# A hybrid SSD / short-convolution block on one core: group-wise scratch tensors, joined transfers, stores on another queue, and a new order at two turns

## The chip, the cores and the metric

The kernel runs on one core of a Trainium2 chip. The metric is device time in microseconds (us), the median of several executions. All arithmetic is float32; matrix products are made of three passes over operands that are split into a high and a low part.

## What is computed

The input x is 1024 tokens by 1024 channels. Cut to what matters here, the reference is:

```python
u = rmsnorm(x) @ w_in                    # 9248 columns in all
z, xbc, dt_raw, s_b, s_c, s_x, g_a, g_b = split(u)
xbc = silu(causal_conv4(xbc) + bias)     # xs 2048, B 4x128, C 4x128
y = ssd_chunked_scan(xs, softplus(dt_raw + bias), a, B, C) + d_skip * xs
y = group_rmsnorm(y * silu(z)) * w       # 4 groups of 512 channels
branch_a = y @ w_ssd_proj
branch_b = (s_b * causal_conv3(s_c * s_x)) @ w_sconv_proj
h = x + (sigmoid(g_a) * branch_a + sigmoid(g_b) * branch_b) @ w_o
h = h + (silu(n(h) @ w_gate) * (n(h) @ w_up)) @ w_down
out = rmsnorm(h)
```

## The kernel before, in words

The order of the instructions on each engine is the order of the program text: nothing is moved by a scheduler. Every wait is a semaphore wait of an engine that works in order. DMAs are issued from three queues: SP's (nearly all loads and most stores), ACT's (a few stores) and POOL's (transfers that add into their target). Working tiles are 47 equal pages of on-chip memory; a new tile takes a page whose last user stands earlier in the program, and waits for that user. Some DMAs also wait for an earlier transfer with other data to land before they are issued (the fourth load of x does): they share a semaphore with it.

The work comes in five stages.

**Start** (`hybrid_block`, lines 225 to 262 and 1487 to 1593). Four row tiles of x are loaded, their squares are summed, the rows are scaled (`rows_scale`, line 129) and transposed on PE; the small weights (`ra`, `rb`) are loaded, transposed (lines 1533 and 1534) and copied into `cols`. Rows 4 to 7 follow as `r1`.

**Pairs.** `x @ w_in` is made in pairs of 128-column blocks, each pair with seven products in place of eight (`Pair`, line 829). A pair has seven slots; a slot is 12 matmuls of 128x512. Operands of x are held as `T["B11"]`, `T["B21"]`, `T["B22"]` and the sums `T["T1"]` to `T["T4"]`. Results go through `silu_z` or `conv_silu`, which run as generators in the list `side`, one step a slot (`pump`), and are stored to DRAM (`z_d`, `xbc_d`) from SP's queue. Meanwhile `weight_sums` makes sums of later weights by DMA alone. `time_steps` (line 286) is the chain for dt; its generator `rest` starts with one empty step.

**Direct tiles with the scans.** The last 22 column blocks (6 of z, 16 gates) are made by `direct_tile` (line 989), 16 turns of three matmuls each, so 352 turns. Between them runs the generator `scans` (line 557), one step each time `pump_scan` is called: first the loads of the first scan inputs (`want`, `prep`), then for each of the 32 items (4 groups by 8 chunks) `part1` and `part2`, 65 steps in all. Each half group ends in a `norm` generator (line 498) of 15 or 18 further steps, advanced one by one with the scan's steps: load of z, product on POOL, squares on ACT, sums on DVE, column sums on PE (`pq`, line 523), the root, a transpose on PE (`prt`, line 528), a small store and a broadcast load back (`rs_d`, `rbc`, lines 532 and 534), scaling (line 540), stores, and for a second half four sums with their stores (line 553).

Ahead of the turn from the pairs to the direct tiles, the loop at line 1652 counts `left`, the slots still to come: at 9 it loads `B12` back, at 8 it makes the scan's first step (the loads), at 6 it loads the first direct slab, at 2 it loads the second, splits the first (`direct_hi`), drops `T2` and starts to split `B12`, at 1 it finishes both and makes the scan's second step. In the direct tiles a scan step is due every 322/65 turns; in the last 30 turns there is a step every third turn, and `every(scan_steps)` runs what is left of the last norm before the next stage.

**Merge and output.** `ms` (line 1158) streams chunks of three products: `gv` (14 chunks), `gy` (28), `go`. A chunk is 24 matmuls; loads run four chunks ahead, splits two. `Merge.first` loads and squashes the gates.

**FFN** (`ffn_phase`) is not touched.

Of the kernel before, what the change touches and what calls it, by code (L numbers as in the profile page):

```python
# [8 lines left out]
F32 = mybir.dt.float32  # L9
# [30 lines left out]
def hybrid_block(ctx: ExitStack, tc: tile.TileContext, x, nmw, w_in, cw, cb, dtb, alog, dsk, snw,  # L40
# [193 lines left out]
    ra = cp.tile([96, P], F32, name="ra")  # L234
    nc.scalar.dma_start(ra, cw[0].rearrange("k (i p) -> (k i) p", p=P))
    rb = cp.tile([80, P], F32, name="rb")
    nc.scalar.dma_start(rb[0:8, :], nmw.rearrange("o (i p) -> (o i) p", p=P))
    nc.scalar.dma_start(rb[8:16, :], nfw.rearrange("o (i p) -> (o i) p", p=P))
    nc.scalar.dma_start(rb[16:40, :], cb.rearrange("o (i p) -> (o i) p", p=P))
    nc.scalar.dma_start(rb[40:56, :], snw.rearrange("o (i p) -> (o i) p", p=P))  # L240
    nc.scalar.dma_start(rb[56:80, :], scw[0].rearrange("k (i p) -> (k i) p", p=P))

# [8 lines left out]
    def small_loads():  # L251
        nc.sync.dma_start(d2, dsk.rearrange("o (i j) -> (o i) j", j=2))
        nc.sync.dma_start(dtbc, dtb.rearrange("o h -> h o"))
        for q in range(4):
            nc.sync.dma_start(al[32 * q:32 * q + 32, :], alog.rearrange("o h -> h o"))
    rd = cp.tile([16, 2, 64], F32, name="rd")
# [11 lines left out]
    e_d = dr.tile([NT, H, P], F32, name="e_d")  # L268
    xbc_d = [dr.tile([P, S], F32, name=f"xbc_d{i}") for i in range(24)]
    z_d = [dr.tile([P, S], F32, name=f"z_d{i}") for i in range(16)]  # L270
    b12_d = dr.tile([2, P, 2, 512], F32, name="b12_d")
    y_g = [dr.tile([512, S], F32, name=f"y_g{i}") for i in range(G)]
    v_g = [dr.tile([512, S], F32, name=f"v_g{i}") for i in range(2)]
    y_d = [y_g[i // 4][i % 4 * P:i % 4 * P + P, :] for i in range(16)]
    v_d = [v_g[i // 4][i % 4 * P:i % 4 * P + P, :] for i in range(KT)]
    ga_d = [dr.tile([P, S], F32, name=f"ga_d{i}") for i in range(KT)]
    gb_d = [dr.tile([P, S], F32, name=f"gb_d{i}") for i in range(KT)]
    rs_d = [dr.tile([4, P], F32, name=f"rs_d{i}") for i in range(2 * G)]
# [7 lines left out]
    def time_steps(ps):  # L286
# [13 lines left out]

        def rest():
            yield
            V.scalar_tensor_tensor(e, u, -1.0, u, op0=ALU.mult, op1=ALU.max)
# [48 lines left out]
    def want(i, part):  # L352


        if i < 2 * G:
            g, o = i // 2, i % 2 * 512
            bcx = [xbc_d[16 + g], xbc_d[20 + g]] + xbc_d[4 * g:4 * g + 4]
            if part < 2:
                t = page("bc", (P, 4, 256))
                for j in range(4):  # L360
                    nc.sync.dma_start(t[:, j, :], bcx[j][:, o + part * 256:o + part * 256 + 256])
            else:
                t = page("x1", HB)
                for j in range(2):
                    nc.sync.dma_start(t[:, j, :], bcx[4 + j][:, o:o + 512])
            halves[i, part] = t
# [131 lines left out]
    def norm(g, hf, y0, y1):  # L498

        ys, o = (y0, y1), slice(hf * 512, hf * 512 + 512)  # L500
        for i in range(2):
            z = page("z", HB)
            for r in range(2):
                nc.sync.dma_start(z[:, r, :], z_d[4 * g + 2 * i + r][:, o])
            if i == 0:
                zs = z
# [31 lines left out]
        for r in range(4):  # L538
            z = ys[r // 2][:, r % 2]
            V.scalar_tensor_tensor(z, z, snc(4 * g + r), rbc, op0=ALU.mult, op1=ALU.mult)  # L540
            if hf == 0 or r > 1:
                nc.sync.dma_start(y_d[4 * g + r][:, o], z)
            if r % 2:
                yield
        if hf == 0:
            kept[g] = ys
            return
# [41 lines left out]
    def conv_silu(i):  # L589

        def f(u):
# [9 lines left out]
            nc.scalar.activation(acc, acc, AF.Silu)  # L601
            nc.sync.dma_start(xbc_d[i], acc)
            yield
        return f

    def silu_z(i):
        def f(u):
            nc.scalar.activation(u, u, AF.Silu)
            nc.sync.dma_start(z_d[i], u)
            yield  # L610
        return f
# [377 lines left out]
    def direct_tile(i):  # L989
# [3 lines left out]
        for hf in range(2):  # L993
            ps = bank("pr")
            for k in range(KT):
                bh, bl = half_b(f"B{k // 4 + 1}{hf + 1}", k % 4)
                mm3(ps, wh[:, k, :], wl[:, k, :], bh, bl, k == 0, k == KT - 1)
                turn[0] += 1
                due = turn[0] * SCAN_STEPS // (len(direct) * 2 * KT - 30)
                if turn[0] > len(direct) * 2 * KT - 30:  # L1000
                    pump_scan(turn[0] % 3 == 0)
                elif due > turn[1]:
                    turn[1] = due
                    pump_scan()
# [13 lines left out]
    class Merge:  # L1018
# [5 lines left out]
        def first(self, c):  # L1024
            n = c.n
            if n not in (2, 7, 3, 4):
                return
            i, j = TO[n]
            if c.k == 0:
                self.g[i, j] = [page("gt", HB) for _ in range(2)]  # L1030
                for m in range(4):
                    nc.sync.dma_start(self.g[i, j][m // 2][:, m % 2, :], self.gd[4 * i + m][:, j * 512:j * 512 + 512])
# [54 lines left out]

    mv = Merge(gb_d, None)
    my = Merge(ga_d, mv.c)

# [9 lines left out]

    def act_blk(d, at):
        def f(f, k, n):
            l, j = int(f[1]) - 1, int(f[2]) - 1

            def ld(t):
                for i in range(n):
                    nc.sync.dma_start(t[:, i, :], d[at(l, k) + i][:, j * 512:j * 512 + 512])
            return ld
        return f

    def fb_v(f, k, n):
        return wfrm(vt_d, f, k, n) if f[0] == "T" else act_blk(v_d, lambda l, k: 4 * l + k)(f, k, n)

    def fb_y(f, k, n):
        return wfrm(yt_d, f, k, n) if f[0] == "T" else act_blk(y_d, yk)(f, k, n)

# [418 lines left out]
    nc.vector.tensor_copy(cols[:, 0:176], pc[:, 0:176])  # L1535
    r0 = rows_scale(*a0, act=(2,), pool=(3,))
    raw0, raw1 = ([], []), ([], [])
# [42 lines left out]
    for k in range(4, 8):  # L1580
        turned_out(raw0, k)
    p1.ev(1)
    every(put("B21", raw0[1]))
    r1 = rows_scale(*a1, act=(2,), pool=(3,))
    p2.ev(1)
# [66 lines left out]
    for i in range(7 * NF, n_slots):  # L1652
# [13 lines left out]
        left = n_slots - 1 - i  # L1666
        if left == 6:
            direct[0][0].load()
        if left == 8:
            pump_scan()  # L1670
        if left == 2:
            direct[1][0].load()
            direct_hi(direct[0][0])
            del T["T2"]
            b12_put = put("B12", b12)
            next(b12_put)
        if left == 9:
            b12 = [page("br", HB) for _ in range(2)]
            for k in range(2):
                nc.sync.dma_start(b12[k], b12_d[k])  # L1680
        if left == 1:
            every(b12_put)
            direct_lo(direct[0][0])
            pump_scan()
    every(sums)
    for f in ("T1", "T3", "T4"):
        del T[f]
    del b12
# [40 lines left out]
```

## Time and profile before

| | us |
|---|---|
| median of 3 runs | 1953.3 |
| lowest, highest | 1949.79, 1953.45 |
| the profiled execution's own time | 1949.93 |
| its span, first to last instruction | 1948.2 |

The page gives each engine's busy time, the granted TensorE clock in 40 slices, the DMA queues and the costliest groups; the views used below are the list of waits (who waited for whom, in total, number of times and longest), the busy time of each engine in a stretch, and the timeline of an engine (start, duration, engine, line, operation, tiles, count, and in brackets the idle time before it and what ended it). Matmul records overlap: one lasts 0.39 us at the full clock while the next starts 0.23 us later.

### The profile page before, as it was taken

How to read it: one execution, taken by the hardware profiler on the slowest of the kernel's cores; microseconds unless marked ns; L12 is line 12 of the kernel's file. 1: busy time of each engine (PE TensorE's matmuls, PEld its weight loads, DVE VectorE, ACT ScalarE, POOL GpSimd, SP SyncE). 2: the span in 40 equal slices, each digit the busy share in tenths (PEclk: the TensorE clock that was granted, in tenths of full speed). 3: DMA queues.
4: the chain of work that ended last, by engine and by line, in shares of the span. 5: the costliest groups of instructions: out<-in, count | busy, mean ns of one | idle time of the engine just before them, and what ended most of it. 6: DMA issues, size and time to landing. Idle time of an engine off the chain costs nothing.

```text
span 1948.2 us, 24338 instructions
## 1 busy us (share of the span) xinstructions
PE 1891.2 (97%) x8917; PEld 1553.1 (80%) x8917; DVE 1291.0 (66%) x1658; ACT 965.8 (50%) x1536; POOL 179.5 (9%) x158
## 2 busy tenths in 40 slices
PE   6999999999997999999989999999999999999998
PEld 5678888888885887888768888888888888888886
DVE  6757877777773778887766557878444444456465
ACT  5545444444445888777546445365333333335333
POOL 0001111011100111011100000101121112100000
PEclk9999999999998999999999999999999999999999
DMA  5187999899957667877778666845988888868552
GB/s 169 37 213 201 224 238 215 232 241 233 260 159 220 190 208 234 268 242 239 227 286 320 213 206 203 224 156 110 232 195 192 213 199 200 207 252 302 195 188 114
DMA packets 347120, 411.99 MB, mean 211 GB/s; under 512 B 19112, under 2 KB 225784, under 8 KB 347000
## 3 DMA queue, kind: packets, MB, share of 16 engines
q1 hardware_dynamic: 300288, 343.23, 54.2%
q0 software_dynamic: 43296, 55.58, 17.8%
q10 hardware_dynamic: 3416, 11.63, 1.5%
q8 instruction: 70, 1.15, 0.2%
q14 instruction: 50, 0.41, 0.1%
HBM read 320.56 MB, written 143.15 MB: 238 GB/s over the span
## 4 chain that ended last, share of the span: by engine, by line
PE 49%; DVE 3%; DMA 2%; ACT 1%; issue 1%; SPq 0%; ACTq 0%; DVEq 0%
PE gb L676 5%; PE gb L675 5%; PE gb L677 5%; PE fb L677 4%; PE fb L676 4%; PE fb L675 4%; PE gd L676 4%; PE gd L677 4%; PE gd L675 4%; PE fd L677 3%; PE fd L676 3%; PE fd L675 3%; PE pr L81 1%; PE pr L83 1%; PE pr L82 1%
## 5 line engine op out<-in xcount | busy, mean ns | idle before, releaser
L77 DVE TENSOR_TENSOR wl<-ws,wh 128x1024 fp32r<-128x1024 f32 x77 | 94.0, 1221 | 121.6 <-ACT wh L76 121.6
L676 PE MATMUL gb<-ql,gh 128*128 128x512 f32 x432 | 168.3, 390 | 3.1 <-DVE ql L77 3.1
L675 PE MATMUL gb<-qh,gh 128*128 128x512 f32 x432 | 168.3, 390 | 1.1 <-DVE h L1133 1.1
L677 PE MATMUL gb<-qh,gl 128*128 128x512 f32 x432 | 168.1, 389 | 0.0
L81 PE MATMUL pr<-th,wh 128*128 128x512 f32 x352 | 146.0, 415 | 7.0 <-ACT wh L983 7.0
L83 PE MATMUL pr<-th,wl 128*128 128x512 f32 x352 | 139.3, 396 | 7.0 <-DVE wl L986 7.0
L82 PE MATMUL pr<-tl,wh 128*128 128x512 f32 x352 | 138.7, 394 | 0.0
L677 PE MATMUL fb<-th,wl 128*128 128x512 f32 x352 | 137.1, 389 | 0.8 <-DVE wl L77 0.8
L675 PE MATMUL fb<-th,wh 128*128 128x512 f32 x352 | 137.1, 390 | 0.6 <-ACT wh L76 0.6
L676 PE MATMUL fb<-tl,wh 128*128 128x512 f32 x352 | 137.0, 389 | 0.0
L675 PE MATMUL gd<-qh,gh 128*128 128x512 f32 x324 | 126.0, 389 | 0.0
L676 PE MATMUL gd<-ql,gh 128*128 128x512 f32 x324 | 126.0, 389 | 0.0
L677 PE MATMUL gd<-qh,gl 128*128 128x512 f32 x324 | 126.0, 389 | 0.0
L76 ACT ACTIVATE qh<-cb 128x1024 fp32r<-128x1024 f32 x98 | 99.9, 1020 | 40.8 <-PE gb L676 19.6
L77 DVE TENSOR_TENSOR ql<-cb,qh 128x1024 fp32r<-128x1024 f32 x98 | 115.5, 1179 | 2.5 <-ACT qh L76 2.4
L74 DVE SCALAR_TENSOR_TENSOR gl<-ca,gh 128x1024 fp32r<-128x1024 f32 (+1 forms) x60 | 70.5, 1174 | 49.7 <-ACT gh L73 49.7
L677 PE MATMUL fd<-th,wl 128*128 128x512 f32 x264 | 102.7, 389 | 0.0
L675 PE MATMUL fd<-th,wh 128*128 128x512 f32 x264 | 102.7, 389 | 0.0
L676 PE MATMUL fd<-tl,wh 128*128 128x512 f32 x264 | 102.7, 389 | 0.0
L676 PEld LDWEIGHTS gb<-ql,gh 128*128 128x128 f32 x432 | 81.1, 188 | 20.7 <-DVE ql L77 4.0
L675 PEld LDWEIGHTS gb<-qh,gh 128*128 128x128 f32 x432 | 81.1, 188 | 18.2 <-DVE h L1133 1.4
L677 PEld LDWEIGHTS gb<-qh,gl 128*128 128x128 f32 x432 | 81.1, 188 | 16.8
(311 smaller groups left out, 4693.3 us busy)
## 6 DMA issues: line engine op xcount, KB each, us to landing
ws<-in_w_in_dram SPq DMA_DIRECT2D x80, 512.0 KB, 8.5
ws<-in_w_gate_dram SPq DMA_DIRECT2D x77, 256.0 KB, 3.5
ws<-in_w_up_dram SPq DMA_DIRECT2D x77, 256.0 KB, 4.4
ca<-u_d SPq DMA_DIRECT2D x35, 512.0 KB, 4.7
ab<-ac_d SPq DMA_DIRECT2D x32, 512.0 KB, 5.3
xbc_d<-cv SPq DMA_DIRECT2D x24, 512.0 KB, 6.7
ws<-ws POOLq DMA_DIRECT2D x22, 512.0 KB, 6.3
wd_d<-in_w_down_dram SPq DMA_DIRECT2D x20, 512.0 KB, 10.7
```

Source lines behind the costliest of these rows:

```text
L74: nc.vector.scalar_tensor_tensor(lo, src, -1.0, hi.bitcast(F32), op0=ALU.mult, op1=ALU.subtract)
L76: nc.scalar.activation(hi, src, AF.Copy)
L77: nc.vector.tensor_sub(lo, src, hi.bitcast(F32))
L81: nc.tensor.matmul(o, lh, rh, start=first, stop=False)
L82: nc.tensor.matmul(o, lh, rl, start=False, stop=False)
L83: nc.tensor.matmul(o, ll, rh, start=False, stop=last)
L675: nc.tensor.matmul(o, lh, rh, start=first, stop=False, skip_group_check=True)
L676: nc.tensor.matmul(o, lh, rl, start=False, stop=False, skip_group_check=True)
L677: nc.tensor.matmul(o, ll, rh, start=False, stop=last, skip_group_check=True)
```

## The change

- `ra` and `rb` (six DMAs) and the small loads (six DMAs) are issued from POOL's queue, not from ACT's and SP's.
- `xbc_d` and `z_d` become slices of one scratch tensor a group, laid out so that one DMA fetches what took four (B, C and two blocks of xs) or two (the other two blocks; two blocks of z); gates, y and v likewise. Stores of `y` go two blocks at a time, a step after they are made.
- Stores from `conv_silu` and `silu_z` are issued from ACT's queue.
- `rest` has three empty steps in place of one.
- Of the row scalings, DVE takes three and ACT one; POOL takes none. For rows 4 to 7 they come before the evictions of the second pair.
- At the turn: `B12` is loaded at 9 as before, the first slab at 7, `B12` is split at 4, the first slab's high part and the second slab's load come at 3, its low part and the scan's first step at 2. `T2`, `T1`, `T3` are dropped at 4, 3, 2. The scan's second step comes in the first direct tile.
- A scan step is due every 348/65 turns to the end; what is left of the last norms runs beside the first eight chunks of `gv`: 4, 3, 0, 3 and then 2 steps a chunk.

```diff
-    nc.scalar.dma_start(ra, cw[0].rearrange("k (i p) -> (k i) p", p=P))
+    nc.gpsimd.dma_start(ra, cw[0].rearrange("k (i p) -> (k i) p", p=P))
...
-        nc.sync.dma_start(dtbc, dtb.rearrange("o h -> h o"))
+        nc.gpsimd.dma_start(dtbc, dtb.rearrange("o h -> h o"))
...
-    xbc_d = [dr.tile([P, S], F32, name=f"xbc_d{i}") for i in range(24)]
-    z_d = [dr.tile([P, S], F32, name=f"z_d{i}") for i in range(16)]
+    xbc_g = [dr.tile([6 * P, S], F32, name=f"xbc_g{i}") for i in range(G)]
+    z_g = [dr.tile([512, S], F32, name=f"z_g{i}") for i in range(G)]
+    z_d = [z_g[i // 4][i % 4 * P:i % 4 * P + P, :] for i in range(16)]
+    xbc_d = [xbc_g[i // 4][(2 + i % 4) * P:(3 + i % 4) * P, :] for i in range(16)] + \
+        [xbc_g[i % 4][i // 4 % 2 * P:i // 4 % 2 * P + P, :] for i in range(16, 24)]
...
         def rest():
             yield
+            yield
+            yield
...
-                for j in range(4):
-                    nc.sync.dma_start(t[:, j, :], bcx[j][:, o + part * 256:o + part * 256 + 256])
+                src = xbc_g[g][0:512, o + part * 256:o + part * 256 + 256]
             else:
                 t = page("x1", HB)
-                for j in range(2):
-                    nc.sync.dma_start(t[:, j, :], bcx[4 + j][:, o:o + 512])
+                src = xbc_g[g][512:768, o:o + 512]
+            nc.sync.dma_start(t, src.rearrange("(j p) l -> p j l", p=P))
...
-            nc.sync.dma_start(xbc_d[i], acc)
+            nc.scalar.dma_start(xbc_d[i], acc)
...
-            nc.sync.dma_start(z_d[i], u)
+            nc.scalar.dma_start(z_d[i], u)
...
-                due = turn[0] * SCAN_STEPS // (len(direct) * 2 * KT - 30)
-                if turn[0] > len(direct) * 2 * KT - 30:
-                    pump_scan(turn[0] % 3 == 0)
-                elif due > turn[1]:
+                due = turn[0] * SCAN_STEPS // (len(direct) * 2 * KT - 4)
+                if due > turn[1]:
...
-    r0 = rows_scale(*a0, act=(2,), pool=(3,))
+    r0 = rows_scale(*a0, act=(3,))
...
+    every(put("B21", raw0[1]))
+    r1 = rows_scale(*a1, act=(3,))
     p1.ev(1)
-    every(put("B21", raw0[1]))
-    r1 = rows_scale(*a1, act=(2,), pool=(3,))
     p2.ev(1)
...
-        if left == 6:
-            direct[0][0].load()
-        if left == 8:
-            pump_scan()
-        if left == 2:
-            direct[1][0].load()
-            direct_hi(direct[0][0])
-            del T["T2"]
-            b12_put = put("B12", b12)
-            next(b12_put)
+        if left in (4, 3, 2):
+            del T[{4: "T2", 3: "T1", 2: "T3"}[left]]
...
-        if left == 1:
-            every(b12_put)
+        if left == 7:
+            direct[0][0].load()
+        if left == 4:
+            every(put("B12", b12))
+        if left == 3:
+            direct_hi(direct[0][0])
+            direct[1][0].load()
+        if left == 2:
             direct_lo(direct[0][0])
             pump_scan()
...
-    every(scan_steps)
     T.clear()
     while ms.at < len(gv.chunks) + len(gy.chunks):
...
         ms.step()
+        pump_scan({1: 4, 2: 3, 3: 0, 4: 3}.get(ms.at, 2))
         pump(2)
         pump_aux()
```

## Rows read from the trace of the kernel before

**Rows 1.** The page, part 1: span and busy time of the engines.
```profile
span 1948.2 us, 24338 instructions
...
PE 1891.2 (97%) x8917; PEld 1553.1 (80%) x8917; DVE 1291.0 (66%) x1658; ACT 965.8 (50%) x1536; POOL 179.5 (9%) x158
```

**Rows 2.** Waits of PE, whole span: us in total, times, longest us.
```profile
PE pt L1543 <- DVE xn L137: 8.8, 4, 6.1
PE pq L523 <- DVE sa L518: 7.7, 2, 6.7
PE pr L81 <- ACT wh L983: 7.0, 1, 7.0
PE pr L83 <- DVE wl L986: 7.0, 3, 6.0
...
PE gb L676 <- DVE ql L77: 3.1, 1, 3.1
```

**Rows 3.** Stretches: length, busy PE, PEld, DVE, ACT, POOL; granted clock; DMA share; GB/s.
```profile
604.00:626.50 22.50, 9.50 (x34) 6.93 (x33) 7.60 (x10) 11.23 (x23) 0.88 (x1) 0.70 0.81 218
970.00:1003.00 33.00, 23.20 (x96) 18.66 (x95) 18.18 (x25) 9.61 (x13) 0.85 (x1) 0.90 0.62 214
129.00:138.00 9.00, 6.12 (x19) 4.27 (x18) 8.79 (x16) 3.74 (x7) 0.87 (x1) 0.81 0.67 120
36.00:43.00 7.00, 5.36 (x21) 4.14 (x20) 6.83 (x11) 3.42 (x5) 1.62 (x1) 0.76 0.01 2
```

**Rows 4.** Timeline of PE about the turn from the pairs to the direct tiles.
```profile
606.82 0.39 PE L676 MATMUL pb<-tl,wk 128*128 128x512 f32 x1
607.04 0.39 PE L677 MATMUL pb<-th,wk 128*128 128x512 f32 x1
...
622.67 0.63 PE L82 MATMUL pr<-tl,wh 128*128 128x512 f32 x1
```

**Rows 5.** Timeline of ACT at the same turn.
```profile
613.32 1.06 ACT L983 ACTIVATE wh<-ws 128x1024 fp32r<-128x1024 f32 x1 [12.81 <-DMA ws<-in_w_in_dram]
```

**Rows 6.** Timeline of SP's queue before that turn.
```profile
587.08 3.11 SPq L361 DMA_DIRECT2D bc<-xbc_d  x4
...
603.37 4.16 SPq L165 DMA_DIRECT2D ws<-in_w_in_dram  x2
```

**Rows 7.** Timeline of DVE in the chain for dt.
```profile
128.27 0.42 DVE L303 SCALAR_TENSOR_TENSOR ts<-ts 128x256 f32<-128x256 f32 x1 [5.03 <-DMA ts<-tr]
```

**Rows 8.** Timeline of ACT, SP, DVE and PE around the last norms.
```profile
963.05 0.27 ACT L530 ACTIVATE rst<-prt 4x128 f32<-4x128 f32 x1 [0.87 <-PE prt L528]
...
970.00 0.32 SPq L532 DMA_DIRECT2D rs_d<-rst  x1
972.64 0.34 SPq L534 DMA_DIRECT2D rbc<-rs_d  x1
...
975.79 1.41 DVE L540 SCALAR_TENSOR_TENSOR y<-y,cols,rbc 128x512 f32<-128x512 f32 x2 [10.26 <-DMA rbc<-rs_d]
...
979.21 1.84 PE L523 MATMUL pq<-ones,sa 128*128 128x1 f32 x8 [6.66 <-DVE sa L518]
```

**Rows 9.** Waits of SP's queue, first 10 us.
```profile
SPq L231 <- DMA x<-in_x_dram: 3.6, 1, 3.6
```

**Rows 10.** Timeline of DVE at the start: the fourth row tile's squares.
```profile
10.70 1.23 DVE L115 SCALAR_TENSOR_TENSOR xn<-x 128x1024 f32<-128x1024 f32 x1 [3.73 <-DMA x<-in_x_dram]
```

**Rows 11.** Line 137, durations in ns: minimum, median, maximum.
```profile
L137 DVE TENSOR_SCALAR xn<-x,nr x4: 753/1185/1621, 13.5 to 36.8; 128x1024 f32<-128x1024 f32 x4
```

**Rows 12.** Tile vt_d: DMA issues on POOL, durations in ns.
```profile
L695 POOL DMA_DIRECT2D vt_d<-v_g x4: 878/878/878, 474.4 to 590.3; - x4
```

**Rows 13.** Tile rb: time from issue to landing.
```profile
DMA to landing us min/median/max: 4.9/4.9/4.9
```

**Rows 14.** Timeline of ACT: the work behind one of its own stores.
```profile
900.79 1.06 ACT L514 ACTIVATE sa<-y 128x1024 f32<-128x1024 f32 x1 [3.68 <-DMA eb<-e_d]
```

**Rows 15.** Waits of SP's queue, whole span.
```profile
SPq L165 <- DMA xbc_d<-cv: 10.5, 3, 5.2
```

More of the change, by code (lines that the diff above doesn't have):

```diff
@@ L234, in hybrid_block @@
     ra = cp.tile([96, P], F32, name="ra")
-    nc.scalar.dma_start(ra, cw[0].rearrange("k (i p) -> (k i) p", p=P))
+    nc.gpsimd.dma_start(ra, cw[0].rearrange("k (i p) -> (k i) p", p=P))
     rb = cp.tile([80, P], F32, name="rb")
[L237 to L241, printed above, removed]
+    nc.gpsimd.dma_start(rb[0:8, :], nmw.rearrange("o (i p) -> (o i) p", p=P))
+    nc.gpsimd.dma_start(rb[8:16, :], nfw.rearrange("o (i p) -> (o i) p", p=P))
+    nc.gpsimd.dma_start(rb[16:40, :], cb.rearrange("o (i p) -> (o i) p", p=P))
+    nc.gpsimd.dma_start(rb[40:56, :], snw.rearrange("o (i p) -> (o i) p", p=P))
+    nc.gpsimd.dma_start(rb[56:80, :], scw[0].rearrange("k (i p) -> (k i) p", p=P))
     def more_loads():
@@ L251, in small_loads @@
     def small_loads():
-        nc.sync.dma_start(d2, dsk.rearrange("o (i j) -> (o i) j", j=2))
-        nc.sync.dma_start(dtbc, dtb.rearrange("o h -> h o"))
+        nc.gpsimd.dma_start(d2, dsk.rearrange("o (i j) -> (o i) j", j=2))
+        nc.gpsimd.dma_start(dtbc, dtb.rearrange("o h -> h o"))
         for q in range(4):
-            nc.sync.dma_start(al[32 * q:32 * q + 32, :], alog.rearrange("o h -> h o"))
+            nc.gpsimd.dma_start(al[32 * q:32 * q + 32, :], alog.rearrange("o h -> h o"))
     rd = cp.tile([16, 2, 64], F32, name="rd")
@@ L273, in hybrid_block @@
     v_g = [dr.tile([512, S], F32, name=f"v_g{i}") for i in range(2)]
-    y_d = [y_g[i // 4][i % 4 * P:i % 4 * P + P, :] for i in range(16)]
+    xbc_d = [xbc_g[i // 4][(2 + i % 4) * P:(3 + i % 4) * P, :] for i in range(16)] + \
+        [xbc_g[i % 4][i // 4 % 2 * P:i // 4 % 2 * P + P, :] for i in range(16, 24)]
     v_d = [v_g[i // 4][i % 4 * P:i % 4 * P + P, :] for i in range(KT)]
-    ga_d = [dr.tile([P, S], F32, name=f"ga_d{i}") for i in range(KT)]
-    gb_d = [dr.tile([P, S], F32, name=f"gb_d{i}") for i in range(KT)]
+    ga_a, gb_a = dr.tile([D, S], F32, name="ga_a"), dr.tile([D, S], F32, name="gb_a")
+    ga_d = [ga_a[i * P:i * P + P, :] for i in range(KT)]
+    gb_d = [gb_a[i * P:i * P + P, :] for i in range(KT)]
     rs_d = [dr.tile([4, P], F32, name=f"rs_d{i}") for i in range(2 * G)]
@@ L356, in want @@
             g, o = i // 2, i % 2 * 512
-            bcx = [xbc_d[16 + g], xbc_d[20 + g]] + xbc_d[4 * g:4 * g + 4]
             if part < 2:
                 t = page("bc", (P, 4, 256))
-                for j in range(4):
-                    nc.sync.dma_start(t[:, j, :], bcx[j][:, o + part * 256:o + part * 256 + 256])
+                src = xbc_g[g][0:512, o + part * 256:o + part * 256 + 256]
             else:
                 t = page("x1", HB)
-                for j in range(2):
-                    nc.sync.dma_start(t[:, j, :], bcx[4 + j][:, o:o + 512])
+                src = xbc_g[g][512:768, o:o + 512]
+            nc.sync.dma_start(t, src.rearrange("(j p) l -> p j l", p=P))
             halves[i, part] = t
@@ L502, in norm @@
             z = page("z", HB)
-            for r in range(2):
-                nc.sync.dma_start(z[:, r, :], z_d[4 * g + 2 * i + r][:, o])
+            nc.sync.dma_start(z, z_g[g][256 * i:256 * i + 256, o].rearrange("(r p) l -> p r l", p=P))
             if i == 0:
@@ L540, in norm @@
             V.scalar_tensor_tensor(z, z, snc(4 * g + r), rbc, op0=ALU.mult, op1=ALU.mult)
-            if hf == 0 or r > 1:
-                nc.sync.dma_start(y_d[4 * g + r][:, o], z)
             if r % 2:
                 yield
+                if hf == 0 or r > 1:
+                    nc.sync.dma_start(y_g[g][128 * (r - 1):128 * (r + 1), o].rearrange("(r p) l -> p r l", p=P),
+                                      ys[r // 2])
         if hf == 0:
@@ L1030, in first @@
                 self.g[i, j] = [page("gt", HB) for _ in range(2)]
-                for m in range(4):
-                    nc.sync.dma_start(self.g[i, j][m // 2][:, m % 2, :], self.gd[4 * i + m][:, j * 512:j * 512 + 512])
+                for m in range(2):
+                    cols_of(self.gd[512 * i + 256 * m:512 * i + 256 * m + 256, :], j, 2)(self.g[i, j][m])
             if c.k == 2:
@@ L1086, in sums @@
                     yield
-    mv = Merge(gb_d, None)
-    my = Merge(ga_d, mv.c)
+    mv = Merge(gb_a, None)
+    my = Merge(ga_a, mv.c)
     def a_raw(w, at):
@@ L1099, in fa_y, with cols_of @@
         return wfrm(ss_d, f, k, n) if f[0] == "S" else a_raw(wssd, yk)(f, k, n)
[L1101 to L1109, printed above, removed]
+    def cols_of(rows, j, n):
+        return lambda t: nc.sync.dma_start(t, rows[:, j * 512:j * 512 + 512].rearrange("(k p) l -> p k l", p=P))
     def fb_v(f, k, n):
-        return wfrm(vt_d, f, k, n) if f[0] == "T" else act_blk(v_d, lambda l, k: 4 * l + k)(f, k, n)
+        if f[0] == "T":
+            return wfrm(vt_d, f, k, n)
+        return cols_of(v_g[int(f[1]) - 1][k * P:(k + n) * P, :], int(f[2]) - 1, n)
     def fb_y(f, k, n):
-        return wfrm(yt_d, f, k, n) if f[0] == "T" else act_blk(y_d, yk)(f, k, n)
+        if f[0] == "T":
+            return wfrm(yt_d, f, k, n)
+        return cols_of(y_g[k // 2][256 * (int(f[1]) - 1):256 * int(f[1]), :], int(f[2]) - 1, n)
     A_IN_C = {"A11": (0, 0), "A12": (1, 0), "A22": (1, 1)}
@@ L1685, in hybrid_block @@
     every(sums)
-    for f in ("T1", "T3", "T4"):
-        del T[f]
-    del b12
+    del T["T4"], b12
     for i in range(len(direct)):
```

## The prediction

> **What bounds the kernel now.** The page comes first: PE is busy for 1891.2 of 1948.2 us [rows 1], and the change leaves PE's work as it is. So a gain can come only from the 57 us in which PE stands and from stretches in which it runs at the lower of its two clock levels (1.2 in place of 2.4 GHz). The list of PE's waits says where it stands: 13.0 us before two matmuls of the first direct tile, 7.7 us before `pq` of a norm, 3.1 us before the second chunk of the merge, 8.8 us before the transposes at the start [rows 2]. The busy times by stretch, taken around these places, show the second half of the loss: the granted clock is 0.70, 0.90, 0.81 and 0.76 of full there [rows 3], and each stretch holds one of those stops. In the timeline a matmul follows the last after 0.23 us at the full clock and its record lasts 0.39 us; in the slow part a record lasts 0.63 us [rows 4], so each costs some 0.2 us more. The tail of the kernel and the short waits in the FFN are not touched.
>
> The sum is made against the profiled execution's own 1949.9 us (span 1948.2 plus 1.7 around it), which stands 3.4 us, or 0.2%, under the median of the runs shown. That is also about what a measurement of this kernel can tell from no change.
>
> **Turn from the pairs to the direct tiles.** PE stops because ACT's split of the first slab starts at 613.3, having waited 12.8 us for the slab to land [rows 5], and then DVE's low part is late, behind the second `B12` split. The slab is asked for at `left` 6, but in SP's queue it stands behind eight loads of the scan's first inputs: these begin at 587.1, the slab's issue at 603.4 [rows 6]. In the change the slab is issued ahead of them, one slot earlier; so it can be asked for some 16 us sooner, at about 587. With the same 9.9 us from issue to use (603.4 to 613.3) it is there at 597, and its split, now at `left` 3, stands in a slot that PE ends at 607.3 - 3 x 2.7 = 599 (12 matmuls x 0.23 = 2.7 us a slot; the last ends at 607.3 [rows 4]). `B12` is split at `left` 4, in pages that `T2` leaves at that slot. Nothing is left for PE to wait on: 13.0 us of idle go, and with them the slow matmuls after it, two before the second stop and some ten after it, 12 x 0.2 = 2.4 us. **Term: -15.4 us**; bounds 0 (slab as late) and -15.4. I take the full value, since 16 us of queue is what separated the request from the issue. What is late next are the scan's first loads, now issued some 14 us later (`left` 2 in place of 8); `part1` of item 0 comes at turn 6, 4 us into the direct tile. That is a rival below.
>
> **Chain for dt.** PE stands 9.0 - 6.1 = 2.9 us between 129 and 138, at a clock of 0.81 [rows 3]. DVE came to the first step of `rest` 5.03 us before `u` had landed [rows 7], and everything queued behind that step on DVE and then ACT was late. Two more empty steps put it two slots, 5.4 us, later in the program, which covers 5.03. The generators behind it in `side` move by 5.4 us too; they only convert and store results. Idle 2.9, slow matmuls 8 x 0.2 = 1.6: **-4.5 us**, bounds -4.5 and 0.
>
> **Start.** The second set of transposes stands 7.0 - 5.4 = 1.6 us idle, at a clock of 0.76 over 7 us [rows 3], which is 2 x 0.24 x 7 = 3.4 us at half speed, half of it lost: 1.6. `r1` now stands ahead of an eviction that waits for PE, so it starts some 2.5 us sooner; both go: -3.2. The scalings themselves move little: with POOL at work beside it DVE's copy took up to 1.62 us, alone 0.75 [rows 11]; three alone are 2.3, as are the two now (1.62 + 0.75). The fourth load of x waited 3.6 us to be issued, for an earlier x load to land [rows 9]; with the six ACT transfers gone from that set it goes at once, and its squares, which start when it lands at 10.7 [rows 10], can start between 0 and 3.6 us sooner; the loads share the same engines, so I take 1.4. Against this, `cols` now waits for six POOL issues: at 0.88 us each [rows 12] the last is issued 4.4 us after the first, and a landing like that of `rb` now is 4.9 us [rows 13], so it lands at 9.3 or later by what POOL does first. Needed is it at 10.7 - 1.4 + 1.2 = 10.5. I take half of the 1.4: -0.7, bounds -3.6 and +1.5. **Term: -3.9 us.**
>
> The Trainium skill speaks here too (DMA: Bandwidth & Descriptors, "Anatomy of one DMA — SWDGE (gpsimd) path"): it gives such a transfer a fixed cost of about 2.0 us plus its bytes. By that estimate `rb` would be in time and the sum 0.7 us lower; no small transfer from POOL is in this trace, so the sum goes by the rows.
>
> **Last norms.** Now: the third last half group's `rst` is ready at 963.1, SP stores it only at 970.0, the broadcast is issued at 972.6, lands at 975.8, and DVE stands 10.3 us on it; the last half's sums are queued behind on DVE, so `pq` waits 6.7 us [rows 2, 8]. After it some eight slow matmuls and a slow `pq` cost 2.4 us, and the burst of scaling and four sums at the end delays the second chunk's split by 3.1 us [rows 2]. Together 12.2 us, which go, because the 18 steps are spread over the merge. But counting the steps puts a stop in their place. At the end of the direct tiles 66 steps are made (one at `left` 2, and 352 x 65/348 rounded down). The four after the first chunk are, for the next to last norm, `prt` with its store and load, two empty ones, and the scaling that needs the load; for the last norm the product, the squares and the sums; its `pq` follows the second chunk. From `rst` to the load's landing is 2.6 + 3.2 us plus 0.6 to get there, and from landing to `pq` 979.2 - 975.8 = 3.4 us [rows 8]: 9.8 us, and PE has 24 x 0.23 = 5.4 us of matmuls in between. So 4.4 us of idle, and about 1.7 us of slow clock as in the chain for dt. **Term: -12.2 + 6.1 = -6.1 us**; bounds -12.2 (something covers it) and -1 (SP as late again as the 6.9 us between 963.1 and 970.0, less what the first chunks' loads leave).
>
> **At nothing.** The joined transfers move the same bytes; SP's issues are not on PE's path once the turn is mended. The 34 stores on ACT (24 of xbc, 10 of z) cost it about 0.3 us each, as SP's now [rows 8], while it is busy for half of the span [rows 1]; and SP no longer stands waiting for ACT. If that cover goes it is the rival below. The gate and y loads run four chunks, 22 us, ahead.
>
> **Sum:** 15.4 + 4.5 + 3.9 + 6.1 = 29.9; 1949.9 - 29.9 = **1920 us**.
>
> **Rivals.**
> (a) *The scan's first loads are late.* Issued at about 601, with 9.9 us as the slab took, they land at 611.5, just when `part1` wants them, and they are 0.75 MB behind a slab of 0.5 MB. For it: the slab took this long. Against it: six transfers become two, so fewer wait for one another. Price: 4 us of idle and 2 of clock, 1926.
> (b) *The norms stop PE as long as before* because SP is again late with `rst`. Six more: 1926. For it speak the chunk loads that share the queue.
> (c) *The norms stop nothing*: 1914. DVE or the load would have to be 4.4 us faster than in rows 8.
> (d) *The slab's landing is a matter of bandwidth, not of its place*: the DMA engines are 81% busy there [rows 3]. Half of the 15.4 stays: 1928.
> (e) *Slower: ACT's stores.* ACT works in order, and a store of its own once held it for 3.68 us until an unrelated transfer had landed [rows 14]; SP stood up to 5.2 us in the same way [rows 15]. In the pairs ACT also makes the evictions and high parts that PE needs about one slot (2.7 us) later. If each of 34 stores held ACT for 3.7 us, PE would lose 1.0 x 34 = 34 us and the gain is gone: that is the point where it decides. At 4.0 us each it is 44 us, 1964. Against it: on 22 such stores in the direct tiles none shows up in PE's waits.
>
> **Chances.** Forecast 0.50 (its own range 1915 to 1925), (a) 0.20, (b) 0.10, (c) 0.06, (d) 0.08, (e) 0.06. The range takes in (a) to (d), the start's bounds and two of the delays together: 1909 to 1937. Faster by over 0.2%: 0.92, all but (e) and a part of unforeseen mixtures; within 0.2%: 0.03; slower: 0.05.
>
> **What would show it.** In the list of PE's waits `pr` after `wh` and `wl` of the direct tiles is gone, as is `u` of line 886; `pq` after `sa` stands at 4 to 5 us, now between the second and third chunk of the merge; the second set of transposes has no wait. The clock is full in all stretches of rows 3 but the last. In ACT's queue stores of `xbc_d` have under 1 us in front of them. Wrong it is if a new wait of over 3 us stands before `pxt` in the first direct tile (a), or if waits for ACT appear within the pairs (e).

## The result, and the profile after

The changed kernel takes 1930.15 us (median of 4 runs, 1929.22 to 1932.89); the kernel before took 1951.55 in the same comparison (4 runs, 1949.77 to 1953.45). The ratio is 0.9893, with a 95% interval of 0.9875 to 0.991: 21.4 us faster. The forecast was 1920, with a range of 1909 to 1937. Direction and range hold; the point is 10 us too low. The profiled execution took 1931.04 us, 11.0 over the forecast, which was made against a profiled execution too.

The page, part 1, of the kernel after: span, and busy time of each engine.

```profile
span 1929.3 us, 24107 instructions
PE 1887.9 (98%) x8917; PEld 1550.9 (80%) x8917; DVE 1291.1 (67%) x1660; ACT 965.0 (50%) x1533; POOL 181.4 (9%) x168
```

Against [rows 1] the engines do the same work; PE's instructions are the same 8917. So the 18.9 us of span are waits and slow clock, as the prediction had it. Where they went is seen by laying the starts of the same matmuls of the two timelines beside each other (us from the start of the span; matmuls are counted from 0, those of the pairs are the ones that write `pb` and `pd`; the last two columns are what each part adds to the difference):

| matmul | before | after | difference | new in this part | forecast |
|---|---|---|---|---|---|
| first transpose of x | 14.35 | 12.77 | -1.6 | -1.6 | -0.7 |
| 100th of the pairs | 59.75 | 54.98 | -4.8 | -3.2 | -3.2 |
| 600th of the pairs | 190.05 | 181.59 | -8.5 | -3.7 | -4.5 |
| last of the pairs | 607.04 | 599.85 | -7.2 | +1.3 | 0 |
| 30th of the direct tiles | 632.56 | 609.93 | -22.6 | -15.4 | -15.4 |
| last of the direct tiles | 993.24 | 961.04 | -32.2 | -9.6 | -9.1 |
| 200th of the merge | 1042.24 | 1022.83 | -19.4 | +12.8 | +3.0 |
| end of the span | 1948.15 | 1929.27 | -18.9 | +0.5 | 0 |

(The last norms' term of -12.2 + 6.1 is split here by place: 12.2 less the 3.1 us that belonged to the merge's second chunk gives -9.1, and 6.1 - 3.1 gives +3.0. Some 2 us of what the merge gives back is `pq` and `prt` themselves, which moved there.) Up to the end of the direct tiles every part came out within 1.3 us, and 32.2 us were gained against some 33 forecast. The merge then gave 12.8 back, where 3.0 were expected. That is nearly the whole miss. Taken together, the two parts with the last norms cost 3.2 us against the kernel before (-9.6 + 12.8), where 6.1 were to be won.

PE's waits, kernel after, whole span (us in total, times, longest us):

```profile
PE pc L1532 <- DMA ra<-in_ssd_conv_w_dram: 7.4, 1, 7.4
PE pq L526 <- DVE sa L521: 6.4, 1, 6.4
PE pt L1542 <- DVE xn L137: 3.2, 3, 2.8
PE gb L680 <- DVE ql L77: 3.2, 1, 3.2
...
PE pr L83 <- DVE wl L990: 2.0, 3, 1.1
...
PE pxt L426 <- DMA x<-xbc_g: 1.4, 1, 1.4
```

Of [rows 2] both 7.0 us waits of the direct tiles are gone (2.0 in three parts are left) and the transposes wait 3.2 in place of 8.8, though 7.4 now stand ahead of them, before the first small transpose, where it was 4.5 before. So the start is judged by the time of the first transpose in the table, not by these waits. The `pq` wait is 6.4 in place of the 4 to 5 announced, and `gb` still waits 3.2: that wait should have gone.

The same stretches as in [rows 3], moved to where that work now lies (turn, last norms, chain for dt, second transposes; columns as there):

```profile
597.00:619.50 22.50, 19.61 (x102) 15.30 (x101) 7.99 (x13) 16.12 (x34) 0.89 (x1) 1.00 1.05 304
961.00:998.00 37.00, 27.45 (x103) 21.95 (x103) 23.93 (x26) 16.37 (x21) 5.70 (x2) 0.82 0.72 248
120.00:138.00 18.00, 18.00 (x82) 14.89 (x81) 14.12 (x25) 5.70 (x9) 2.34 (x3) 1.00 1.04 247
33.00:40.00 7.00, 6.60 (x36) 5.24 (x35) 6.86 (x12) 2.82 (x6) 0.00 (x0) 1.00 0.14 56
```

Three of the four are mended: full clock, and 102 matmul records in the turn's 22.5 us where there were 34. The second is as bad as it was, only later: a granted clock of 0.82, with PE busy for 27.5 of 37 us.

**The stop in the merge, read from the timelines.** First POOL, then DVE, kernel after, from the first merge matmul on:

```profile
963.53 5.70 POOL L513 TENSOR_TENSOR y<-y,z 128x1024 f32<-128x1024 f32 x2 [33.34 <-ACT gh L73]
```

```profile
963.56 3.47 DVE L74 SCALAR_TENSOR_TENSOR gl<-ca,gh 128x1024 fp32r<-128x1024 f32 x1 [4.12 <-ACT gh L73]
966.95 3.37 DVE L77 TENSOR_TENSOR ql<-cb,qh 128x1024 fp32r<-128x1024 f32 x1
970.24 1.21 DVE L77 TENSOR_TENSOR gl<-ca,gh 128x1024 fp32r<-128x1024 f32 x1
971.38 1.21 DVE L77 TENSOR_TENSOR ql<-cb,qh 128x1024 fp32r<-128x1024 f32 x1
972.51 1.22 DVE L557 TENSOR_TENSOR y<-y,s 128x1024 f32<-128x1024 f32 x1
981.55 1.41 DVE L543 SCALAR_TENSOR_TENSOR y<-y,cols,rbc 128x512 f32<-128x512 f32 x2 [7.82 <-DMA rbc<-rs_d]
```

DVE's first two splits last 3.47 and 3.37 us, the next two, of the same shape, 1.21: the long ones are those beside which POOL multiplies `y` by `z` of the last half group (963.5 to 969.2). Some 4.4 us are lost on DVE, and `ql`, which PE needs for the second chunk, is late. `T4`'s sum of the group before (L557) comes only at 972.5.

The small store of the next to last norm, ACT and then SP, kernel after:

```profile
967.01 0.27 ACT L533 ACTIVATE rst<-prt 4x128 f32<-4x128 f32 x1 [0.64 <-PE prt L531]
```

```profile
973.75 0.36 SPq L558 DMA_DIRECT2D yt_d<-y  x1
974.21 0.32 SPq L535 DMA_DIRECT2D rs_d<-rst  x1
976.58 0.35 SPq L537 DMA_DIRECT2D rbc<-rs_d  x1
```

`rst` is ready at 967.3, but SP stands behind the store of `T4` until 973.75. So the small store leaves at 974.2, 6.9 us late (in [rows 8] it is 6.7, from 963.32, where `rst` ends, to 970.00), and DVE stands 7.8 us on the broadcast.

PE, kernel after:

```profile
966.73 0.47 PE L679 MATMUL gb<-qh,gh 128*128 128x512 f32 x1
970.37 0.80 PE L680 MATMUL gb<-ql,gh 128*128 128x512 f32 x1 [3.17 <-DVE ql L77]
970.96 0.63 PE L681 MATMUL gb<-qh,gl 128*128 128x512 f32 x1
...
976.36 0.39 PE L679 MATMUL gb<-qh,gh 128*128 128x512 f32 x1
...
984.97 1.84 PE L526 MATMUL pq<-ones,sa 128*128 128x1 f32 x8 [6.38 <-DVE sa L521]
986.67 0.78 PE L679 MATMUL gd<-qh,gh 128*128 128x512 f32 x1
987.24 0.63 PE L680 MATMUL gd<-ql,gh 128*128 128x512 f32 x1
```

Two stops, 3.17 and 6.38 us, and behind each a run of matmuls at 0.43 us apart, the half clock. What they cost: the first 48 merge matmuls took 986.67 - 961.27 = 25.4 us, and the next 24 another 1.6 more than before; 48 x 0.23 is 11.0. So 14.4 + 1.6 = 16.0 us, of which 9.55 are idle and 6.4 are slow matmuls and `pq` itself. The forecast had 6.1.

### The profile page after: what moved, and what is told of

Same layout as the page of the kernel before. It is cut to its first block, busy times and chain, and to the rows that moved or that the text cites. A ratio compares the mean times of both kernels' runs of the same rounds, so it can differ in the third digit from the quotient of the medians.

```text
span 1929.3 us, 24107 instructions
## 1 busy us (share of the span) xinstructions
PE 1887.9 (98%) x8917; PEld 1550.9 (80%) x8917; DVE 1291.1 (67%) x1660; ACT 965.0 (50%) x1533; POOL 181.4 (9%) x168
## 4 chain that ended last, share of the span: by engine, by line
PE 87%; DVE 6%; ACT 3%; DMA 2%; issue 1%; SPq 0%; ACTq 0%; DVEq 0%
PE pb L679 5%; PE pb L680 5%; PE pb L681 5%; PE gb L680 5%; PE gb L679 5%; PE gb L681 5%; PE fb L681 4%; PE fb L679 4%; PE fb L680 4%; PE pr L81 4%; PE pr L83 4%; PE gd L679 4%; PE gd L680 4%; PE gd L681 4%; PE pr L82 4%; PE pd L679 4%
```

## The experiments

Each is an edit of the kernel after. Ratios are to the kernel before, with their 95% intervals; four runs each unless said.

### The merge: who stops PE

**The last product on DVE in place of POOL.**

```diff
-            nc.gpsimd.tensor_mul(y, y, z)
+            (V if (g, hf) == (G - 1, 1) else nc.gpsimd).tensor_mul(y, y, z)
```

> The changed kernel with the last half group's product y*z made on DVE in place of POOL, nothing else. Theory A (POOL's product beside DVE's splits stretches those splits, and the late DVE then holds SP's queue before the small store): DVE's splits of the second merge chunk take 1.2 us again, PE's stop of 3.2 us there and the slow stretch after it (about 3.4 us lost) go, the store of rst is issued some 4 us sooner and the stop before pq falls from 6.4 to 4 us or less: about 1921 to 1923 us. Theory B (the stop before pq is only the round trip of the small store and the broadcast load, whatever POOL does): the stop before pq stays at 6 us or grows; about 1924 to 1926 us.

Measured: 1927.22 us, 0.9879 (0.9865 to 0.9894), which is slower than either theory gave. The first stop is gone, and the splits are short again. DVE and then SP of this kernel:

```profile
962.84 1.23 DVE L74 SCALAR_TENSOR_TENSOR gl<-ca,gh 128x1024 fp32r<-128x1024 f32 x1 [4.11 <-ACT gh L73]
...
977.83 1.41 DVE L543 SCALAR_TENSOR_TENSOR y<-y,cols,rbc 128x512 f32<-128x512 f32 x2 [6.95 <-DMA rbc<-rs_d]
```

```profile
968.64 0.36 SPq L558 DMA_DIRECT2D yt_d<-y  x1
969.09 0.32 SPq L535 DMA_DIRECT2D rs_d<-rst  x1
972.88 0.35 SPq L537 DMA_DIRECT2D rbc<-rs_d  x1
```

So the first stop is POOL's work beside DVE. But only 2.9 us are won: `pq`'s stop grew from 6.38 to 9.54. The small store still leaves behind `T4`'s, at 969.1; it is 2.5 us late (`rst` is ready at 966.57 here) in place of 6.9. From there to the landing of the broadcast it is 977.8 - 969.1 = 8.7 us. PE came to `pq` sooner and waited longer.

**The steps spread more evenly over the merge's chunks**, and **both edits together.**

```diff
-        pump_scan({1: 4, 2: 3, 3: 0, 4: 3}.get(ms.at, 2))
+        pump_scan({1: 2, 2: 2, 5: 2}.get(ms.at, 1))
```

> The changed kernel with the 17 steps left of the norms spread thinner over the merge: 2, 2, 1, 1, 2 and then 1 a chunk, so that two chunks (11 us) lie between the small transpose and the scaling that waits for its broadcast, and pq comes two chunks later. Theory A and B: the 6.4 us before pq and the slow clock after it (about 3.4 us lost) go, the 3.2 us before the second chunk stay: about 1920 us. A rival C (the merge has no slack: the same DVE work in it delays the splits wherever it stands, so the stop only moves): 1928 to 1931 us, with new waits for DVE's high and low parts in later chunks.

> Both edits, the product on DVE and the thinner steps. Theory A: both stops and both slow stretches go, 3.2 + 6.4 + 2 x 3.4 = 16.4 us: about 1914 us. If the gains overlap (B or C): 1920 to 1924 us.

Measured: spread 1925.19, 0.9869 (0.9852 to 0.9885); both 1923.39, 0.9858 (0.9843 to 0.9873). Spread alone came out between its two expectations: it leaves the first stop at 3.12 and halves the other to 3.11. With both, the first is gone. In both kernels the row of PE of the second has another releaser; with both edits it is:

```profile
987.31 1.87 PE L526 MATMUL pq<-ones,sa 128*128 128x1 f32 x8 [4.73 <-DVE mc L1052]
```

`sa` is in time here; `pq` waits for a bank of PSUM that DVE empties for the merge (`mc`). So there is a third cause once the first two are gone: `pq` takes its turn among the merge's own banks. That is the releaser as the trace infers it. It was not tried alone, but the next kernel makes `pq` at another place among the chunks, and its wait falls to 0.4 us.

**One step a chunk, two only at the fifth and sixth**, so that `pq` falls between other evictions, with the product on DVE, and the same steps with the product left on POOL.

```diff
-        pump_scan({1: 4, 2: 3, 3: 0, 4: 3}.get(ms.at, 2))
+        pump_scan({5: 2, 6: 2}.get(ms.at, 1))
```

> The changed kernel with the last product on DVE and the 17 steps one a chunk, two at the fifth and sixth, so that pq and the small transpose fall where four PSUM banks are free (between the second product's evictions and the fourth's start). Theory A' (three causes stand behind the merge's stops: POOL beside DVE, the round trip of the small store and the broadcast load inside too few chunks, and pq wanting a bank that DVE has yet to empty): no stop over 1 us and no slow stretch from the end of the direct tiles to the FFN, 16 us less than the changed kernel: about 1914 us. Rival C (the merge has no room for this work on DVE): a new wait for DVE's low parts, 1920 us or more.

> The kernel with the steps spread as in the fifth run, but the last product on POOL as in the changed kernel. Theory A' (POOL beside DVE stretches the splits): a stop of about 3 us before the second merge chunk and a slow stretch of 3 us or more behind it are back, 5 to 6.5 us over the fifth run: about 1921 us. Rival (with the steps spread there is room for it): 1916 to 1917 us.

Measured: 1915.84 with the product on DVE, 0.9821 (0.9805 to 0.9837), and 1919.96 with it on POOL, 0.9837 (0.9821 to 0.9853). The stretch of the merge, first on DVE, then on POOL (columns as above), and DVE of the second:

```profile
961.00:998.00 37.00, 36.04 (x164) 29.24 (x163) 29.11 (x35) 24.33 (x29) 0.00 (x0) 1.00 0.84 300
```

```profile
961.00:998.00 37.00, 33.99 (x142) 27.68 (x141) 26.90 (x23) 21.67 (x24) 5.70 (x2) 0.91 0.78 285
```

```profile
964.15 3.31 DVE L74 SCALAR_TENSOR_TENSOR gl<-ca,gh 128x1024 fp32r<-128x1024 f32 x1 [4.11 <-ACT gh L73]
967.39 3.37 DVE L77 TENSOR_TENSOR ql<-cb,qh 128x1024 fp32r<-128x1024 f32 x1
970.68 1.21 DVE L77 TENSOR_TENSOR gl<-ca,gh 128x1024 fp32r<-128x1024 f32 x1
```

With the product on DVE it is the best of all, 14.3 us below the kernel after and 34.6 below the kernel before in its own comparison (1950.42): its direct tiles end where those of the kernel after do (first merge matmul at 961.30 against 961.27), and its first 48 merge matmuls take 11.01 us, full speed. The pair differs by the engine of two multiplications alone, and those cost 4.1 us on POOL (3.6 when each kernel is taken against the kernel before of its own comparison): `gb` waits 3.0 for `ql`, and the clock falls after it. With the product on POOL only the first stop is there and `pq` does not wait, so the two stops have causes of their own.

**The end of the scans as before** (a step every third turn, and the rest run to the end ahead of the merge).

```diff
-                due = turn[0] * SCAN_STEPS // (len(direct) * 2 * KT - 4)
-                if due > turn[1]:
+                due = turn[0] * SCAN_STEPS // (len(direct) * 2 * KT - 30)
+                if turn[0] > len(direct) * 2 * KT - 30:
+                    pump_scan(turn[0] % 3 == 0)
+                elif due > turn[1]:
...
+    every(scan_steps)
     T.clear()
```

> The changed kernel with the end of the scans as it was before: a step due every 322/65 turns, one every third turn in the last 30, and all that is left run before the merge. Theory A (moving the last norm beside the merge is a loss in this form: it cost 12.2 us where it stood and costs 16 us now): about 1926 us, with a stop before pq in the direct tiles of 5 to 7 us. The forecast's own account (the move is worth 6 us): about 1936 us.

Measured: 1936.28, 0.9923 (0.9908 to 0.9938), 6.1 us slower than the kernel after. PE's waits of this kernel:

```profile
PE pq L526 <- DVE sa L521: 10.6, 2, 9.0
...
PE gb L680 <- DVE ql L77: 3.9, 1, 3.9
```

I had come to suspect that moving the last norms was no gain at all, or a loss. Under the new turn it is a gain of 6 us, the very net that the forecast gave it. But this agreement is luck: the old end costs more here than in the kernel before (a stop of 9.0 in place of 6.7, and the direct tiles from the 30th matmul on take 367.5 us in place of 360.7), so the net agrees by two sizes that were both too small. Against the kernel before, the move is the loss of 3.2 us above. One difference from the kernel before remains in this edit: the turn makes one scan step where there were two, so one more is left for the end. Whether that makes its stop longer was not tried.

### The turn, undone alone

The slots of `left` are put back as they were (loads, splits and scan steps, with the count of steps due lowered by the one that is made ahead of the direct tiles again; joined transfers and ACT's stores stay).

```diff
+        if left == 6:
+            direct[0][0].load()
+        if left == 8:
+            pump_scan()
...
-        if left == 7:
-            direct[0][0].load()
-        if left == 4:
-            every(put("B12", b12))
-        if left == 3:
-            direct_hi(direct[0][0])
...
```

> The changed kernel with the turn as before: the scan's loads at 8 slots to go, the first slab at 6, its split and B12's at 2 and 1; joined transfers and stores on ACT stay. Forecast's account (the place of the slab in SP's queue made the stop): six loads stand ahead of it in place of eight, so most of the stop is back, 8 to 13 us, about 1940 us. Rival (fewer and larger transfers and free stores alone mended it): 1930 to 1933 us.

Measured: 1948.24 (10 runs), 0.9988 (0.9979 to 0.9998): 18.1 us slower than the kernel after and 8 slower than was expected of it. Its first merge matmul starts at 977.07, 15.8 later. PE's waits and ACT's split in this kernel:

```profile
PE pr L83 <- DVE wl L990: 6.8, 2, 6.5
PE pr L81 <- ACT wh L987: 5.1, 1, 5.1
```

```profile
607.96 1.06 ACT L987 ACTIVATE wh<-ws 128x1024 fp32r<-128x1024 f32 x1 [12.76 <-DMA ws<-in_w_in_dram]
```

With the old order the slab is asked for at 592.5, behind the scan's first inputs (579.7 to 592.4), and the waits of [rows 2, 5] are back, though the loads are joined: 11.9 us in place of 14.0. From the last matmul of the pairs to the 30th of the direct tiles this kernel takes 23.1 us; the kernel before took 25.5, the kernel after 10.1, and the twelve kernels with the new order lie between 7.8 and 11.8. So at that place the order is worth 13.0 of the 15.4; what wins the other 2.4 without it (the joins, or ACT's stores) was not separated. A further 3.3 us are lost in the pairs just ahead of the turn, which the next section comes back to. The kernel after, ACT and SP (the first two slabs, of which the first is asked for at 579.8, and then the scan's first inputs):

```profile
598.69 1.06 ACT L987 ACTIVATE wh<-ws 128x1024 fp32r<-128x1024 f32 x1 [5.57 <-DMA ws<-in_w_in_dram]
```

```profile
579.79 7.27 SPq L165 DMA_DIRECT2D ws<-in_w_in_dram  x2
587.81 7.38 SPq L369 DMA_DIRECT2D bc<-xbc_g  x1
```

Here the forecast was right with little to spare. The slab did not take 9.9 us from issue to use but 598.7 - 579.8 = 18.9, and the split ended at 599.75 with PE's first direct matmul at 600.08.

### The chain for dt: two parts that each do it

One empty step again; the stores of `xbc` and `z` back on SP; and both.

```diff
             yield
-            yield
-            yield
             V.scalar_tensor_tensor(e, u, -1.0, u, op0=ALU.mult, op1=ALU.max)
...
-            nc.scalar.dma_start(xbc_d[i], acc)
+            nc.sync.dma_start(xbc_d[i], acc)
...
-            nc.scalar.dma_start(z_d[i], u)
+            nc.sync.dma_start(z_d[i], u)
```

> The changed kernel with one empty step in the chain for dt in place of three. Forecast's account: DVE waits some 5 us for u, PE stands 2 to 3 us and runs slow for 3.4: about 1934 to 1935 us. Rival (SP, free of stores, brings u early enough): 1930 us, no wait.

> The changed kernel with the stores of xbc and of the first ten z blocks on SP's queue again. Forecast's account (the move to ACT is worth nothing by itself): 1929 to 1932 us. Rival (they free SP, and the loads' lead hangs on it): a stop at the turn or in the pairs comes back, 1935 us or more.

> The changed kernel with one empty step in the chain for dt and the stores of xbc and z on SP's queue, both as before. Theory D (each of the two alone mends that stop: the empty steps by waiting, the freed queue by bringing u sooner): the stop of 2 to 3 us and its slow stretch are back, with a wait of DVE for u of 4 to 5 us: 1934 to 1935 us. Rival (the stop went for another reason, such as the earlier start): no stop, 1930 us.

Measured: 1931.33, 0.9902 (0.9887 to 0.9917); 1929.75, 0.9891 (0.9876 to 0.9906); 1932.65, 0.9905 (0.989 to 0.9919). Neither edit alone can be told from the kernel after. Both together are 2.5 us slower, with intervals that overlap, but the trace decides: DVE's wait in the third kernel, from 90 to 150 us, is the old one of [rows 7] to a tenth of a microsecond:

```profile
DVE ts L307 <- DMA ts<-tr: 4.9, 1, 4.9
```

With the stores on ACT alone (one empty step) that wait is 2.5 us, with the empty steps alone 0.6. So the forecast named one of two parts that each nearly suffice. How the stores' move does it is not the queue's order: `u`'s transfer is issued as soon as ACT has made its data in all these kernels, for which SP stands waiting. SP of the kernel with one empty step, then of the one with both undone:

```profile
114.20 2.46 SPq L301 DMA_DIRECT2D ts<-tr  x4
```

```profile
114.58 2.46 SPq L301 DMA_DIRECT2D ts<-tr  x4
```

But DVE uses the data at 121.21 in the first, 7.0 us after the first issue, and at 124.06 in the second, 9.5 us after it; in the kernel before it was 9.6. In this pair the transfer lands sooner with the stores on ACT; why is not shown. From the 300th to the 600th matmul of the pairs the four kernels show it: 70.6 us after, 71.3, 70.0, and 74.2 with both undone, against 74.3 before.

The third kernel came out 2 us under what the theory gave, and the rest of the pairs tells why: from the 600th to the last it takes 416.2 to 417.0 us in the three kernels with the stores on SP (before, and these two), and 418.2 to 419.1 in ten kernels with them on ACT; in the eleventh, with the turn undone, 421.6. So ACT's stores do cost the pairs 1.2 us or more, in no single wait of PE that the lists show. That is the direction of rival (e), at a small part of its price; which mechanism makes it is not shown. With the stores on SP the turn gives most of it back: there `z`'s stores stand in SP's queue ahead of the first slab (the third kernel's stores begin at 582.9, its slab is asked for at 587.0), and PE waits 1.2 and 1.3 us for the slab's split before its first direct matmul, which has no wait in the kernel after. A store that itself held ACT, and through it PE, shows in the kernel with the turn undone:

```profile
588.19 0.60 ACT L890 ACTIVATE u<-pb 128x512 f32<-128x512 f32 x1 [3.83 <-DMA br<-b_d]
```

ACT's store of `z`, the next in its order, stood there for an unrelated landing, and PE stopped for 1.8 us. In the kernel after nothing of the kind is seen: ACT is idle for 0.03 us in front of every store of `xbc` and for at most 1.0 in front of one of `z`, so the forecast's sign (under 1 us) held, and what the stores cost the pairs is not their own waiting.

### Parts that the forecast put at little or nothing

The small loads back on ACT's and SP's queues, and every joined transfer cut up into single ones (the layout kept).

```diff
-            nc.sync.dma_start(t, src.rearrange("(j p) l -> p j l", p=P))
+            for j in range(src.shape[0] // P):
+                nc.sync.dma_start(t[:, j, :], src[j * P:j * P + P, :])
...
```

> The changed kernel with the twelve small loads on ACT's and SP's queues as before. Forecast's account (they made the fourth load of x wait): that load is issued 3 to 4 us later again, the first transposes start 1.2 to 1.8 us later, about 1931.5 to 1932 us. Rival (the start was bound by the DMA engines): no difference, 1930 us.

> The changed kernel with the joined transfers of xbc, z, y, v and the gates made one by one again; layout, order and queues stay as changed. Forecast's account (they move the same bytes and SP is not on PE's path once the turn is mended): 1929 to 1933 us. Rival (the small transfers wait for one another, as the scan's first loads did before): a stop of 3 us or more before the first transposes of the scan or in the norms, 1935 us or more.

Measured: 1930.12, 0.9893 (0.9878 to 0.9907), and 1929.88, 0.9891 (0.9876 to 0.9906). Neither can be told from the kernel after. The first was expected to lose 1.5 us if the start's term was right. Its first transpose starts at 13.67, the latest of all the changed kernels, but the twelve others, with the loads on POOL, lie between 12.54 and 13.63: the term of 0.7 is smaller than what varies from one profiled run to the next, and stays open. Its mechanism is seen, however: the fourth load of x waits 3.9 us to be issued here, as it did in [rows 9], and not at all in the kernel after. What that brings is small: the squares of that tile start at 10.03 here, at 9.12 in the kernel after and at 9.71 in the kernel with single transfers, whose load does not wait either.

## Why the prediction was right, and which term was mis-sized

**Turn: right**, -15.4 forecast and measured, of which 13.0 go when the order alone is undone. The exact agreement is partly luck, since the same stretch varies from 7.8 to 11.8 us in the kernels with the new order. The latency in the forecast was wrong (9.9 us from issue to use; 18.9 measured) and the 16 us of head start covered that with about 0.3 us over. Rival (d) was thus half true, without a price. Rival (a) shows as the 1.4 us wait of `pxt`.

**Chain for dt: right in place and nearly in size** (-3.7 for -4.5); the cause was half seen, since the stores' move does nearly the same work.

**Start: right in place and size for `r1`** (-3.2, from the first transpose to the 100th matmul of the pairs), though `r1` and the row scalings were not undone alone. For x and `rb` the sum went by a landing of 4.9 us [rows 13], and the rows of POOL and PE, kernel after, agree:

```profile
4.55 0.53 POOL L241 DMA_DIRECT2D rb<-in_sconv_w_dram  x1
```

```profile
9.58 0.37 PE L1533 MATMUL pc<-ident,rb 80*128 80x80 f32 x1 [1.83 <-DMA rb<-in_sconv_w_dram]
```

From the last issue to use it is 5.0 us. The 2.0 us that the Trainium skill gives as fixed cost (DMA: Bandwidth & Descriptors, "Anatomy of one DMA — SWDGE (gpsimd) path") is not what this row shows, with x's loads under way beside it.

**Last norms: the step that failed.** The forecast counted one stop of 4.4 us and 1.7 of slow clock, from 2.6 + 3.2 us of transfers that start when `rst` is ready. Measured were 16.0 us, and the whole term came out at +3.2 for -6.1, outside its bounds of -12.2 and -1; the total stayed in the range because the other terms held. Three things stood in its place. (1) A price that was not in the sum at all: POOL's product beside DVE's splits, 4.1 us with its clock, shown by the pair of kernels that differ in that alone. (2) SP was late with `rst` by 6.9 us, the case of rival (b) and the end of the bound; but what held SP was not the chunk loads that the rival named, but `T4`'s store ahead of it in the queue, whose sum DVE makes late. (3) Store and broadcast took 7.3 us (974.2 to 981.55) and 8.7 in the kernel with the product on DVE, where the sum had 5.8. The forecast had looked at each step's own duration and not at what else shares DVE's operands and SP's queue in those few chunks. What (2) and (3) make can be added up in the kernel with the product on DVE: SP is 2.5 us late there and the transfers take 8.7 - 5.8 = 2.9 more than the sum had; with the forecast's 4.4 that gives 9.8, and the stop measured 9.54. In the kernel after, the first stop and its slow matmuls cover a part of them. Together with `pq`'s bank they are what spreading the steps takes away.

**At nothing: right for the joins and, in the total, for ACT's stores**; in the pairs these cost 1 to 2 us, most of which the turn gives back.

Had the last norms cost nothing in the merge, the time would have been 1930 - 14 = 1916 (the 16.0 less some 2 us of `pq` and `prt`, which have to be made somewhere): that is the best kernel above, and close to rival (c).

## What to carry to other kernels

Work moved off one stage is paid in the stage that it goes to: list, for the few microseconds where it lands, what else stands in each queue ahead of it and who reads its operands beside it, before giving it a price. A small store in front of a load that an engine waits for should not be issued behind a store whose data are made later. And where a change has several parts, undo them one at a time and in pairs: here two parts did nearly the same work, and undoing one showed almost nothing.

## What the runs showed of the hardware that was not expected

DVE's splits with both inputs in on-chip memory took 1.21 to 1.23 us alone and 3.31 to 3.47 beside a POOL multiplication that reads such memory too; the second ended 1.1 us after POOL's last (970.3 against 969.2), as if it had waited for all of it. The Trainium skill has this rule (SBUF — State Buffer, "Who interferes with whom": a DVE instruction with two inputs in SBUF, which is this memory, contends with one of GpSimd, here POOL, that reads SBUF). The runs agree, and give it a size: 2.1 to 2.3 us an instruction here.

A stop of 3.17 us was followed by 13 matmuls at half the clock in the kernel after. In the kernel before, one of 3.15 us at nearly the same place was followed by none; PE's timeline of that kernel:

```profile
1002.44 0.50 PE L676 MATMUL gb<-ql,gh 128*128 128x512 f32 x1 [3.15 <-DVE ql L77]
1002.77 0.39 PE L677 MATMUL gb<-qh,gl 128*128 128x512 f32 x1
```

Eleven kernels have this stop, of 2.9 to 3.9 us. Three of them (the kernel before, the turn undone, one empty step) show no slow matmul between it and the next stop, six show 7 or 8, and two (the kernel after, and the one with one step a chunk and the product on POOL) show 13. So what a stop costs in clock can't be read from its length alone, and a price that holds a stop's clock, like the 4.1 us above, is that of one case; what tells the cases apart was not tried.
